# Layer norm without weights on one core: an in-place ring of 48 rows, and two-pass statistics on three engines

## The chip, the cores and the metric

The kernel runs on one core of one Trainium2 chip. The metric is the device time of one execution in microseconds; the number for a kernel is the median over its runs. Of the core's engines three compute here: VectorE (DVE in the profile), ScalarE (ACT) and GpSimd (POOL). SyncE (SP) and ScalarE issue DMAs. TensorE does nothing in either version.

## The reference

Every one of the 32 x 512 = 16384 vectors of 1024 fp32 numbers is brought to mean 0 and variance 1:

```python
def reference(x: np.ndarray, eps: float) -> np.ndarray:
    mean = np.mean(x, axis=-1, keepdims=True)
    var = np.var(x, axis=-1, keepdims=True)
    return ((x - mean) / np.sqrt(var + eps)).astype(np.float32)
```

x has the shape 32 x 512 x 1024, eps is 1e-5. 67.11 MB are read and 67.11 MB written.

## The kernel before

The 16384 vectors are cut into 128 "rows" of 128 vectors, one vector to each partition. A row is thus a 128x1024 piece of 0.52 MB, and a tile is K such rows: 15 tiles of 8 rows (4.19 MB each), then one of 4 and two of 2 rows. A tile is loaded by one DMA, and stored by one.

Input tiles go into `xr`, a ring of 32 rows, and results into `yr`, a ring of 16 rows, so up to four tiles of 8 are loaded ahead and two are on their way out. The instructions of each engine stand in the order in which the program writes them (`manual_schedule`); semaphores between engines and DMAs are set from the tiles that they read and write. Loads are issued on SP's queue, stores on ScalarE's.

For each tile `group` does the following:

- VectorE takes statistics over half rows of 512 elements (`bn_stats`, L77), two to a row, 16 to a tile of 8.
- GpSimd combines these half-row results into the sum of squared deviations and the negated mean, with nine small operations on at most 32 elements a partition (L66 to L102).
- ScalarE takes the square root (L105), VectorE the reciprocal (L109), GpSimd the product of negated mean and reciprocal (L111).
- ScalarE normalises each row (L113), from `xr` to `yr`, and issues the tile's store (L129).

A load into `xr` (L124) waits until ScalarE has read the rows that it overwrites; L113 waits until the store of the rows of `yr` that it overwrites has landed. What the change touches is all of `group`, the two rings, and the loop at the end of the kernel.

Of the kernel before, what the change touches and what calls it, by code (L numbers as in the profile page):

```python
# [1 line left out]

# [4 lines left out]


TILES = (8, 8, 8, 8, 8, 8, 8, 8, 8, 8, 8, 8, 8, 8, 8, 4, 2, 2)  # L10

XRING = 32
YRING = 16

GROUP = 8


def place(tiles, ring):

    plan, row, pos = [], 0, 0  # L20
    for K in tiles:
        if pos + K > ring:
            pos = 0
        plan.append((K, row, pos))
        row += K
        pos += K
    return plan


@with_exitstack  # L30
def kernel(
    ctx: ExitStack,
    tc: tile.TileContext,
    x: bass.AP,
    eps: bass.AP,
    out: bass.AP,
):
    nc = tc.nc
    P = nc.NUM_PARTITIONS
    eps_val = float(eps) if not isinstance(eps, bass.AP) else 1e-5  # L40

    x2 = x.flatten_outer_dims()
    o2 = out.flatten_outer_dims()
    N, D = x2.shape
    BN_MAX = nc.vector.BN_STATS_FMAX
    NSUB = D // BN_MAX
    assert sum(TILES) * P == N

    rings = ctx.enter_context(tc.tile_pool(name="rings", bufs=1))
    st = ctx.enter_context(tc.tile_pool(name="st", bufs=4))  # L50

    fdt = mybir.dt.float32
    AF = mybir.ActivationFunctionType
    ALU = mybir.AluOpType

    xr = rings.tile([P, XRING, D], fdt)
    yr = rings.tile([P, YRING, D], fdt)
    eps_t = rings.tile([P, 1], fdt)

    def rows_of(a, row, K):  # L60
        return a[row * P : (row + K) * P].rearrange("(p k) d -> p k d", p=P)

    def pool_sum(o, terms):
        G = terms.shape[1]
        half = st.tile([P, GROUP, 2], fdt, name="half")
        nc.gpsimd.tensor_tensor(  # L66
            out=half[:, :G], in0=terms[:, :, 0:2], in1=terms[:, :, 2:4], op=ALU.add
        )
        nc.gpsimd.tensor_tensor(  # L69
            out=o, in0=half[:, :G, 0], in1=half[:, :G, 1], op=ALU.add  # L70
        )

    def group(xs, ys, G):
        stats = st.tile([P, GROUP, NSUB, 6], fdt, name="stats")
        for k in range(G):
            for s in range(NSUB):
                nc.vector.bn_stats(  # L77
                    out=stats[:, k, s, :],
                    in_=xs[:, k, s * BN_MAX : (s + 1) * BN_MAX],
                )  # L80

        H = 2 * NSUB
        parts = stats[:, :G].rearrange("p g s (h c) -> p g (s h) c", h=2)
        mean4, m2 = parts[:, :, :, 1], parts[:, :, :, 2]
        nmean = st.tile([P, GROUP], fdt, name="nmean")
        dev = st.tile([P, GROUP, H], fdt, name="dev")
        ss = st.tile([P, GROUP], fdt, name="ss")
        pool_sum(nmean[:, :G], mean4)
        nc.gpsimd.tensor_scalar(  # L89
            out=nmean[:, :G], in0=nmean[:, :G], scalar1=-1.0 / H, scalar2=None, op0=ALU.mult  # L90
        )
        nc.gpsimd.tensor_tensor(  # L92
            out=dev[:, :G],
            in0=mean4,
            in1=nmean[:, :G].unsqueeze(2).to_broadcast([P, G, H]),
            op=ALU.add,
        )
        nc.gpsimd.tensor_mul(out=dev[:, :G], in0=dev[:, :G], in1=dev[:, :G])  # L98
        nc.gpsimd.tensor_scalar(  # L99
            out=dev[:, :G], in0=dev[:, :G], scalar1=float(D // H), scalar2=None, op0=ALU.mult  # L100
        )
        nc.gpsimd.tensor_tensor(out=dev[:, :G], in0=dev[:, :G], in1=m2, op=ALU.add)  # L102
        pool_sum(ss[:, :G], dev[:, :G])
        std = st.tile([P, GROUP], fdt, name="std")
        nc.scalar.activation(  # L105
            out=std[:, :G], in_=ss[:, :G], func=AF.Sqrt, bias=eps_t, scale=1.0 / D
        )
        rstd = st.tile([P, GROUP], fdt, name="rstd")
        nc.vector.reciprocal(out=rstd[:, :G], in_=std[:, :G])  # L109
        nmr = st.tile([P, GROUP], fdt, name="nmr")  # L110
        nc.gpsimd.tensor_mul(out=nmr[:, :G], in0=nmean[:, :G], in1=rstd[:, :G])  # L111
        for k in range(G):
            nc.scalar.activation(  # L113
                out=ys[:, k, :],
                in_=xs[:, k, :],
                func=AF.Identity,
                bias=nmr[:, k : k + 1],
                scale=rstd[:, k : k + 1],
            )

    with tc.manual_schedule():
        nc.vector.memset(eps_t, eps_val)  # L122
        for (K, row, xp), (_, _, yp) in zip(place(TILES, XRING), place(TILES, YRING)):
            nc.sync.dma_start(out=xr[:, xp : xp + K, :], in_=rows_of(x2, row, K))  # L124
            for g in range(0, K, GROUP):
                G = min(GROUP, K - g)
                a, b = xp + g, yp + g
                group(xr[:, a : a + G, :], yr[:, b : b + G, :], G)
            nc.scalar.dma_start(out=rows_of(o2, row, K), in_=yr[:, yp : yp + K, :])  # L129


# [1 line left out]
_INS = ['x', 'eps']  # L133
_OUTS = [((32, 512, 1024), 'float32')]

_NUMBERS = {'eps': 1e-05}


# [26 lines left out]
```

## Time and profile before

| | us |
|---|---|
| median of 12 runs (318.09 to 319.24) | 318.46 |
| the profiled execution's own time | 318.93 |
| its span, first to last instruction | 317.2 |
| time around the span | 1.7 |
| first load, issue to landing | 12.3 |
| a load of 4 MiB, issue to landing, median | 34.4 |
| a store of 4 MiB, issue to landing, median | 29.4 |

The page gives busy time for each engine, then 40 equal slices of the span with the busy share in tenths, the share of the 16 DMA engines and the rate in GB/s. A landing time holds the time in which a DMA shares the DMA engines with others in flight. The groups list, for each line of the kernel and operation, the shape, the count, the sum of the durations, the mean of one, and the idle time of the engine ahead of them with what ended it. A mean can be longer than the spacing, because one instruction's end overlaps the next one's start.

### The profile page before, as it was taken

Reading aid. Unit: us, or ns where it says so; the run is one execution under the profiler, and the core shown is the slowest. Engines: PE = TensorE matmul, PEld = TensorE weight load, DVE = VectorE, ACT = ScalarE, POOL = GpSimd, SP = SyncE. Lnnn points to the kernel's source line nnn. Section 1 sums busy time; section 2 is a strip of 40 time slices with the busy share of each in tenths; the row PEclk is TensorE's granted clock in tenths of the full one; section 3 lists DMA queues with packets and bytes.
Section 4 is the critical chain, followed back from the end, with each engine's and each line's share of the span. In section 5 each row is a group of like instructions: output and inputs, shape, how many; then the busy total and the mean of one; then the engine's idle time right before and its main releaser. Section 6 shows DMA issues by size and latency. Waiting matters only on the chain.

```text
span 317.2 us, 749 instructions
## 1 busy us (share of the span) xinstructions
DVE 155.6 (49%) x275; ACT 153.4 (48%) x147; POOL 41.2 (13%) x184
## 2 busy tenths in 40 slices
DVE  0387595709256191652907438083480925650330
ACT  1007591290833809247091651906529074759651
POOL 0011202200202002020020200102011020202220
DMA  8999999999999999999999999999999999999996
GB/s 331 409 450 434 413 402 438 430 430 430 434 427 446 417 426 443 434 430 442 426 434 426 434 434 439 422 442 434 430 434 426 438 434 432 432 422 439 421 413 257
DMA packets 5189, 134.26 MB, mean 423 GB/s; under 512 B 576, under 2 KB 576, under 8 KB 576
## 3 DMA queue, kind: packets, MB, share of 16 engines
q1 hardware_dynamic: 2592, 67.11, 49.6%
q10 hardware_dynamic: 2592, 67.11, 49.1%
q14 instruction: 5, 0.04, 0.0%
HBM read 67.11 MB, written 67.11 MB: 423 GB/s over the span
## 4 chain that ended last, share of the span: by engine, by line
DMA 64%; ACT 23%; DVE 7%; POOL 2%; issue 1%; ACTq 0%; POOLq 0%
DMA out_dram<-yr 61%; ACT yr L113 22%; DVE stats L77 7%; DMA xr<-in_x_dram 4%; POOL half L66 0%; ACT std L105 0%; POOL dev L99 0%; POOL dev L102 0%; POOL dev L92 0%; POOL nmean L89 0%; POOL dev L98 0%; POOL nmean L69 0%; POOL ss L69 0%; DVE rstd L109 0%; ACTq L129 0%
## 5 line engine op out<-in xcount | busy, mean ns | idle before, releaser
L113 ACT ACTIVATE yr<-xr,nmr,rstd 128x1024 f32<-128x1024 f32 x128 | 146.7, 1226 | 118.3 <-DMA out_dram<-yr 116.2
L77 DVE BATCH_NORM_STATS2 stats<-xr 128x6 f32<-128x512 f32 x256 | 153.3, 676 | 12.2 <-DMA xr<-in_x_dram 12.2
L109 DVE RECIPROCAL rstd<-std 128x8 f32<-128x8 f32 (+2 forms) x18 | 3.5, 197 | 138.9 <-ACT std L105 138.9
L66 POOL TENSOR_TENSOR half<-stats 128x16 f32<-128x16 f32 (+2 forms) x18 | 4.1, 230 | 161.3 <-DVE stats L77 161.3
L105 ACT ACTIVATE std<-ss,eps_t 128x8 f32<-128x8 f32 (+2 forms) x18 | 5.4, 300 | 37.4 <-POOL ss L69 31.4
L111 POOL TENSOR_TENSOR nmr<-nmean,rstd 128x8 f32<-128x8 f32 (+2 forms) x18 | 3.6, 200 | 93.2 <-DVE rstd L109 93.2
L99 POOL TENSOR_SCALAR dev<-dev 128x32 f32<-128x32 f32 (+2 forms) x18 | 5.2, 290 | 1.6
L102 POOL TENSOR_TENSOR dev<-dev,stats 128x32 f32<-128x32 f32 (+2 forms) x18 | 4.5, 250 | 1.5
L92 POOL TENSOR_TENSOR dev<-stats,nmean 128x32 f32<-128x32 f32 (+2 forms) x18 | 4.3, 237 | 1.5
L98 POOL TENSOR_TENSOR dev<-dev 128x32 f32<-128x32 f32 (+2 forms) x18 | 4.2, 233 | 1.4
L89 POOL TENSOR_SCALAR nmean<-nmean 128x8 f32<-128x8 f32 (+2 forms) x18 | 4.1, 229 | 1.6
L66 POOL TENSOR_TENSOR half<-dev 128x16 f32<-128x16 f32 (+2 forms) x18 | 3.8, 212 | 1.4
L69 POOL TENSOR_TENSOR nmean<-half 128x8 f32<-128x8 f32 (+2 forms) x18 | 3.6, 200 | 1.4
L69 POOL TENSOR_TENSOR ss<-half 128x8 f32<-128x8 f32 (+2 forms) x18 | 3.6, 200 | 1.4
L105 ACT ACT_TABLE_LOAD x1 | 1.3, 1283 | 0.9 <-DVE eps_t L122 0.9
L122 DVE MEMSET eps_t<- 128x1 f32 x1 | 0.1, 59 | 0.8 <-PEq L146 0.8
L146 POOL MEMSET const-float32-0.0<- 128x1 f32 x1 | 0.1, 98 | 0.2 <-issue 0.2
L146 POOL MEMSET const-bfloat16-1.0<- 128x1 bf16 x1 | 0.1, 101 | 0.0
L146 POOL MEMSET const-uint8-127<- 128x1 uint8 x1 | 0.1, 101 | 0.0
L146 POOL MEMSET const-float32-1.0<- 128x1 f32 x1 | 0.1, 98 | 0.0
## 6 DMA issues: line engine op xcount, KB each, us to landing
xr<-in_x_dram SPq DMA_DIRECT2D x15, 4096.0 KB, 34.4
out_dram<-yr ACTq DMA_DIRECT2D x15, 4096.0 KB, 29.4
xr<-in_x_dram SPq DMA_DIRECT2D x1, 2048.0 KB, 34.0
xr<-in_x_dram SPq DMA_DIRECT2D x2, 1024.0 KB, 47.0
out_dram<-yr ACTq DMA_DIRECT2D x1, 2048.0 KB, 10.1
out_dram<-yr ACTq DMA_DIRECT2D x2, 1024.0 KB, 7.4
```

Source lines behind the costliest of these rows:

```text
L66: nc.gpsimd.tensor_tensor(out=half[:, :G], in0=terms[:, :, 0:2], in1=terms[:, :, 2:4], op=ALU.add)
L69: nc.gpsimd.tensor_tensor(out=o, in0=half[:, :G, 0], in1=half[:, :G, 1], op=ALU.add)
L77: nc.vector.bn_stats(out=stats[:, k, s, :], in_=xs[:, k, s * BN_MAX : (s + 1) * BN_MAX],)
L89: nc.gpsimd.tensor_scalar(out=nmean[:, :G], in0=nmean[:, :G], scalar1=-1.0 / H, scalar2=None, op0=ALU.mult)
L92: nc.gpsimd.tensor_tensor(out=dev[:, :G], in0=mean4, in1=nmean[:, :G].unsqueeze(2).to_broadcast([P, G, H]), op=ALU.add,)
L98: nc.gpsimd.tensor_mul(out=dev[:, :G], in0=dev[:, :G], in1=dev[:, :G])
L99: nc.gpsimd.tensor_scalar(out=dev[:, :G], in0=dev[:, :G], scalar1=float(D // H), scalar2=None, op0=ALU.mult)
L102: nc.gpsimd.tensor_tensor(out=dev[:, :G], in0=dev[:, :G], in1=m2, op=ALU.add)
L105: nc.scalar.activation(out=std[:, :G], in_=ss[:, :G], func=AF.Sqrt, bias=eps_t, scale=1.0 / D)
L109: nc.vector.reciprocal(out=rstd[:, :G], in_=std[:, :G])
L111: nc.gpsimd.tensor_mul(out=nmr[:, :G], in0=nmean[:, :G], in1=rstd[:, :G])
L113: nc.scalar.activation(out=ys[:, k, :], in_=xs[:, k, :], func=AF.Identity, bias=nmr[:, k : k + 1], scale=rstd[:, k : k + 1],)
```

## The change

Two things are changed together.

**Ring and queues.** One ring of 48 rows replaces `xr` and `yr`; results are written over the inputs. The tiles are now 4, 4, fourteen of 8, then 6 and 2 rows. Loads are issued on ScalarE's queue, stores on SP's. Seven loads go out at the start (48 rows). Each later load is issued behind the work of the tile two after the last owner of its rows (`BEHIND`): behind tile t the load of tile t+4, which waits for the store of tile t-2.

**Statistics and normalisation.** The first two tiles and the last three (`bn`) take half-row statistics on VectorE, which also combines them (`bn_aggr`). The thirteen tiles between (`two_pass`) do it in two passes: VectorE sums each row (L65), GpSimd scales the sums to the negated mean (L71), ScalarE squares the deviation of every row (L76), for six of the rows into PSUM and for two with an accumulated sum, VectorE adds up the squares in PSUM (L89), ScalarE takes the root (L98), VectorE the reciprocal (L101). The rows are normalised on GpSimd (L103, L147), and only in the last two tiles on ScalarE. On each engine a tile's instructions still stand behind those of the tile before: in the program as built GpSimd's list repeats one L71 and eight L103, VectorE's two L65, three L89 and one L101, ScalarE's eight L76, one L98 and, from the fourth tile, one load.

```diff
-TILES = (8, 8, 8, 8, 8, 8, 8, 8, 8, 8, 8, 8, 8, 8, 8, 4, 2, 2)
-
-XRING = 32
-YRING = 16
-
-GROUP = 8
...
+TILES = (4, 4) + (8,) * 14 + (6, 2)
+
+RING = 48
+
+
+HEAD, TAIL = 2, 3
+
+BEHIND = 2
...
+    st = ctx.enter_context(tc.tile_pool(name="st", bufs=2))
+    sm = ctx.enter_context(tc.tile_pool(name="sm", bufs=len(TILES)))
+    ps = ctx.enter_context(tc.tile_pool(name="ps", bufs=2, space=bass.MemoryType.PSUM))
...
+    ring = rings.tile([P, RING, D], fdt)
+    junk = rings.tile([P, D], fdt)
...
+    def two_pass(xs, K):
+
+        sums, ssq, std, rstd, nmean = map(small, ("sums", "ssq", "std", "rstd", "nmean"))
+        half = K // 2
+        for a in (0, half):
+            nc.vector.tensor_reduce(
+                out=sums[:, a : a + half],
+                in_=xs[:, a : a + half, :],
+                axis=AX.X,
+                op=ALU.add,
+            )
+        nc.gpsimd.tensor_scalar(
+            out=nmean[:, :K], in0=sums[:, :K], scalar1=-1.0 / D, scalar2=None, op0=ALU.mult
         )
...
+        def square(o, k, total=None):
+            nc.scalar.activation(
+                out=o,
+                in_=xs[:, k, :],
+                func=AF.Square,
+                bias=nmean[:, k : k + 1],
+                scale=1.0,
+                accum_out=total,
+            )
+
+        def chunk(k):
+            sq = ps.tile([P, 2, D], fdt, name="sq")
+            for i in range(2):
+                square(sq[:, i, :], k + i)
+            nc.vector.tensor_reduce(
+                out=ssq[:, k : k + 2], in_=sq, axis=AX.X, op=ALU.add
+            )
+
+        chunk(0)
+        chunk(2)
+        for k in range(6, K):
+            square(junk, k, ssq[:, k : k + 1])
+        chunk(4)
+        nc.scalar.activation(
+            out=std[:, :K], in_=ssq[:, :K], func=AF.Sqrt, bias=eps_t, scale=1.0 / D
         )
...
+        nc.vector.reciprocal(out=rstd[:, :K], in_=std[:, :K])
+        for k in range(K):
+            nc.gpsimd.tensor_scalar(
+                out=xs[:, k, :],
+                in0=xs[:, k, :],
+                scalar1=nmean[:, k : k + 1],
+                scalar2=rstd[:, k : k + 1],
+                op0=ALU.add,
+                op1=ALU.mult,
+            )
+
+    def bn(xs, K, on_scalar):
...
+            nc.vector.bn_aggr(out=mv[:, k, :], in_=stats[:, k, :, :])
...
+        for k in range(K):
+            if on_scalar:
+                nc.scalar.activation(
+                    out=xs[:, k, :],
+                    in_=xs[:, k, :],
+                    func=AF.Identity,
+                    bias=nmr[:, k : k + 1],
+                    scale=rstd[:, k : k + 1],
+                )
+            else:
+                nc.gpsimd.tensor_scalar(
+                    out=xs[:, k, :],
+                    in0=xs[:, k, :],
+                    scalar1=mv[:, k, 0:1],
+                    scalar2=rstd[:, k : k + 1],
+                    op0=ALU.subtract,
+                    op1=ALU.mult,
+                )
...
+    after, owner = [], {}
+    for t, (K, row, pos) in enumerate(plan):
+        before = [owner[r] for r in range(pos, pos + K) if r in owner]
+        after.append(max(before) + BEHIND if before else -1)
+        owner.update((r, t) for r in range(pos, pos + K))
+
+    def load(done):
+        for t, (K, row, pos) in enumerate(plan):
+            if after[t] == done:
+                nc.scalar.dma_start(
+                    out=ring[:, pos : pos + K, :], in_=rows_of(x2, row, K)
+                )
 
     with tc.manual_schedule():
...
+        load(-1)
+        nc.gpsimd.memset(eps_t, eps_val)
+        for t, (K, row, pos) in enumerate(plan):
+            xs = ring[:, pos : pos + K, :]
+            left = len(TILES) - t
+            if t < HEAD or left <= TAIL:
+                bn(xs, K, on_scalar=left <= 2)
+            else:
+                two_pass(xs, K)
+            nc.sync.dma_start(out=rows_of(o2, row, K), in_=xs)
+            load(t)
```

## The prediction

> **What bounds the kernel now.** I read the page's head and its slices first, then the windows of engine busy time with the DMA share, then the chain of waits, then the groups by form.
>
> ```profile
> span 317.2 us, 749 instructions
> DVE 155.6 (49%) x275; ACT 153.4 (48%) x147; POOL 41.2 (13%) x184
> DMA  8999999999999999999999999999999999999996
> GB/s 331 409 450 434 413 402 438 430 430 430 434 427 446 417 426 443 434 430 442 426 434 426 434 434 439 422 442 434 430 434 426 438 434 432 432 422 439 421 413 257
> ```
>
> No engine is busy half of the span; the DMA engines are full in every slice but the first and the last. The windows (length, then DVE, ACT and POOL busy us, clock, DMA share, GB/s) agree:
>
> ```profile
> 120.00:160.00 40.00, 19.40 (x34) 20.17 (x20) 5.56 (x25) 1.00 1.00 433
> 300.00:317.00 17.00, 2.74 (x6) 6.35 (x7) 2.24 (x11) 1.00 0.81 344
> ```
>
> The plateau is 433 GB/s at share 1.00. A tile of 8 rows moves 4.19 MB in and 4.19 MB out, so a tile costs 8.39 / 0.433 = 19.4 us of DMA. All 134.26 MB cost 310 us, and the span is only 7 us more. The chain says the same, and its first piece gives the latency of a first load:
>
> ```profile
> DMA 64%; ACT 23%; DVE 7%; POOL 2%; issue 1%; ACTq 0%; POOLq 0%
> ...
> 0.72 12.29 DMA xr<-in_x_dram
> ```
>
> The load's 4.19 MB take 9.7 us at the plateau, so 2.6 us are fixed. Prices of the work, by form:
>
> ```profile
> L113 ACT ACTIVATE yr<-xr,nmr,rstd 128x1024 f32<-128x1024 f32 x128 | 146.7, 1226 | 118.3 <-DMA out_dram<-yr 116.2 <-POOL nmr L111 2.1
> L105 ACT ACTIVATE std<-ss,eps_t 128x8 f32<-128x8 f32 x15 | 4.5, 301 | 34.3 <-POOL ss L69 29.0 <-ACT yr L113 5.2
> L77 DVE BATCH_NORM_STATS2 stats<-xr 128x6 f32<-128x512 f32 x256 | 153.3, 676 | 12.2 <-DMA xr<-in_x_dram 12.2
> L109 DVE RECIPROCAL rstd<-std 128x8 f32<-128x8 f32 x15 | 3.0, 203 | 122.8 <-ACT std L105 122.8
> L99 POOL TENSOR_SCALAR dev<-dev 128x32 f32<-128x32 f32 x15 | 4.5, 299 | 1.3
> L89 POOL TENSOR_SCALAR nmean<-nmean 128x8 f32<-128x8 f32 x15 | 3.5, 231 | 1.3
> L89 POOL TENSOR_SCALAR nmean<-nmean 128x2 f32<-128x2 f32 x2 | 0.4, 220 | 0.2
> L99 POOL TENSOR_SCALAR dev<-dev 128x16 f32<-128x16 f32 x1 | 0.3, 257 | 0.1
> ```
>
> VectorE's 256 statistics come every 0.60 us (153.3 / 256), ScalarE's rows every 1.146 us (146.7 / 128); the longer means are single latencies. In each 19.4 us tile both have about 9 us to spare: a compute chain is free until it needs more than 19.4 us a tile.
>
> **What the Trainium skill says.** "ScalarE: Activation LUTs", section "What ACT_TABLE_LOAD costs": an ACTIVATE takes 186 ns + 0.833 ns an element, each pointer operand 93 ns more, and neighbours overlap by 93 ns. L113 has two pointers: 186 + 186 + 853 = 1225, and the trace has 1226; it agrees. "VectorE: DVE Perf Modes", "The perf-mode tier table": a tensor_reduce runs at one element a cycle (0.96 GHz) for any type. L77 agrees for its operation: 512 elements are 533 ns, so the spacing holds 64 ns of overhead. "GPSIMD Engine Reference", "Elementwise — side-by-side cycle accounting": a loop body with up to two operations is port-bound at 1.03 cycles an element at 1.2 GHz, a tight unrolled loop 1.8 cycles (512 elements in 769 ns). The trace has only tiny tensors. "SBUF — State Buffer", "Who interferes with whom": a tensor_reduce never contends with GpSimd; nothing in the trace tests it.
>
> **The change, part by part.**
>
> *Loads, ring and stores.* 48 rows may be on chip, loads go out on ScalarE's queue, stores on SP's. Seven loads (48 rows) are issued at once, 7 x 0.36 us (stores on ScalarE's queue now take 338 to 374 ns each), plus the table load of 1.28 us: done by about 4.5 us, before tile 0 has landed, so nothing. Tile 0 (4 rows, 2.1 MB) lands at 0.72 + 2.6 + 4.8 = 8.2 us, tile 1 at 13.0, tile 2 at 22.7. Later loads are issued behind the square root of tile t for tile t+4 and wait for store t-2, which went out more than a period before; alone it needs about 12 us, under traffic 29.4 us now. So the wait should be over. If not, the next tile's squares on ScalarE stand behind it and the excess is paid in full. A load has three periods to land.
>
> *Statistics.* The 180 small POOL operations, the 256 half-row statistics and 128 ScalarE normalisations mostly go. All sat beside DMA, so their removal gains nothing by itself. In their place thirteen tiles (2 to 14) get a cycle through three engines, in strict program order on each: VectorE sums tile t+1 only after tile t's reciprocal; GpSimd scales t+1's sums (nmean) only after it has normalised all 8 rows of t; ScalarE's squares need nmean; the reciprocal needs the squares. So from reciprocal to reciprocal there is one serial loop, with only one overlap: the sums (VectorE) beside the normalisation (GpSimd).
> - Sums: 2 x (4096/0.96 + 64 ns) + 0.08 = 8.74 us. From below 7.5, from above 9.6 (L77's 1.17 ns an element).
> - nmean: 0.23 (L89) + 0.07 = 0.30 us.
> - Eight squares, one pointer fewer than L113: 1.13 us alone, 1.04 back to back. Every second one in the built program waits for the one before it, 1.18 with the wait. 4 x 1.04 + 4 x 1.18 = 8.9, and two accumulator reads, not in the trace, 0 to 0.2 us each, taken at 0.2: 9.3 us. Bounds 8.3 to 9.9.
> - Last reduction, 2048 elements from PSUM: 2.13 + 0.2 + 0.05 = 2.4 us. The first two hide under later squares.
> - Square root 0.30, reciprocal 0.20, handing over 0.1: 0.6 us.
>
> The loop without its overlapped pair is 0.3 + 9.3 + 2.4 + 0.6 = 12.6 us, so the period is T = 12.6 + max(8.74, 8c), c being GpSimd's time for one 128x1024 row with two pointers. Even with c at nothing T is 21.3, over the 19.4 of DMA: the kernel stops being DMA-bound, whatever c is.
>
> *The price c.* The skill's port bound gives 0.88 + 0.2 (L89's fixed part) = 1.08 us. Its 1.8-cycle loop gives 1.54 + about 0.17 = 1.7. The trace's one-dimensional slope, (231 - 220)/6 = 1.83 ns an element, gives 2.1; L99's slope, (299 - 257)/16 = 2.63, gives 2.9, but L99 runs over rows of four, whose loop starts may be most of it. I take 1.7: the small rows exclude neither end, yet none shows a slope near 0.86 ns. It is an estimate from the page on GPSIMD. 8c = 13.6, T = 26.2.
>
> *Head.* Tile 0: eight statistics 4.8, four aggregations (not in the trace; 0.06 to 0.3, taken as the reciprocal's 0.2), then 0.6: 14.4. Tile 1 the same, 20.6. GpSimd finishes both by 28, under the sums of tile 2 (22.7 to 31.4). Reciprocal of tile 2: 31.4 + 12.6 = 44. Of tile 14: 44 + 12 x 26.2 = 358.5.
>
> *Tail.* Tile 15's statistics end 11.9 later, at 370.4 (16 x 0.6 + 8 x 0.2 + 0.7), but GpSimd is on tile 14 until 372.1 and normalises tile 15 until 385.7. Tiles 16 and 17 are normalised on ScalarE: 370.4 + 9.1 + 7.0 = 386.5 and 389, so they wait for nothing. Then 8.39 MB of stores remain: 19.4 + 2.6 = 22. Span 407.7; around the span lie 318.93 - 317.2 = 1.7 us. Sum 409 us. The sum is made against the profiled 318.93; the median 318.46 is 0.5 lower, far below the errors here. In short: 409 = 219 + 112c for c above 1.5.
>
> **Rivals.**
> *B: GpSimd at its port rate, VectorE's sums close the loop.* c = 1.08, T = 21.3: tile 14's reciprocal at 299.7, tile 15's statistics 311.6, normalised 320.3, stores 22.4: 342.7 + 1.7 = 344 us. For it: the skill's port bound; against it: the slopes of L89 and L99.
> *C: GpSimd much slower.* c = 2.1: 454 us. c = 2.9: 219 + 325 + 6 (tiles 0 and 1 then hold up nmean of tile 2) = 550 us. For it: L99's slope; against it: rows of four elements.
> *D, the other side: VectorE reduces at two elements a cycle.* Sums 4.4 instead of 8.74 and the last reduction 1.3 instead of 2.4: T = max(4.4, 8c) + 11.5. It decides from T below 19.4, that is with c below 1.0. Then DMA sets the pace: reciprocal 14 at about 38 + 12 x 19.4 = 271, 11.9 and 8 for tile 15, 22.4 for stores: 313 + 1.7 = 315 us. Against it: the skill's one element a cycle, L77's rate, and the need for c below every estimate.
>
> **How the numbers follow.** The chosen case (c 1.4 to 2.0, 376 to 443 us) 0.46; B with c up to 1.4 (335 to 376) 0.27; C (over 443) 0.23; D 0.04. The prediction is 409. The range, 338 to 458, covers the chosen case, almost all of B and the near part of C. The lead of the slow cases is structural: the serial loop needs over 19.4 us for any c. Faster by over 0.2% 0.03, within 0.2% (about what a measurement of this kernel can tell) 0.01, slower 0.96.
>
> **What would show it.** In the profile after: the DMA share below 1.0 in the middle slices; ScalarE's squares waiting for nmean thirteen times, about 8c + 0.6 us each; nmean starting right behind the eighth normalised row (in B, behind the sums); the spacing of the normalising rows reads c, that of the reciprocals T. I am wrong if the reciprocals come every 19.4 us with DMA full; if nmean runs ahead of the normalisation; or if ScalarE stands at a load's wait for a store.

## The result, and the profile after

The kernel after takes 385.08 us (median of 8 runs, 385.01 to 385.19), the kernel before in the same series 318.39 us: 1.2091 times as long (interval 1.2081 to 1.2102). The profiled execution's span is 383.4 us. Its page begins, with the columns of before:

```profile
span 383.4 us, 595 instructions
DVE 237.0 (62%) x157; ACT 131.8 (34%) x157; POOL 185.6 (48%) x138
DMA  8999999999899999999998999999898090720397
GB/s 313 450 434 436 395 434 438 438 379 421 349 428 376 400 401 363 390 379 383 379 390 379 424 397 362 403 362 403 345 421 383 0 438 0 321 116 0 144 415 317
```

There are fewer instructions and still no engine is full, yet DMA no longer sets the pace: the rate lies about 385 GB/s through the middle and falls to nothing in three slices near the end. That most digits remain 9 is a trap: a 9 stands for 90% or more, so the tenths hide a loss of one part in ten. The window that stood at 433 GB/s and a share of 1.00 before has now

```profile
120.00:160.00 40.00, 29.27 (x12) 15.11 (x18) 19.23 (x18) 1.00 0.94 381
```

The rate has fallen by more than the share, so it is the GB/s that tells. The chain has turned over. DMA held 64% of it; now:

```profile
POOL 44%; ACT 27%; issue 13%; DVE 8%; DMA 2%; POOLq 1%; ACTq 0%
```

Who waited for whom (total us, times, longest):

```profile
POOL ring L103 <- DVE rstd L101: 156.9, 13, 12.1
ACT sq L76 <- POOL nmean L71: 144.4, 13, 24.5
DVE ssq L89 <- ACT sq L76: 87.9, 26, 17.0
...
DVE mv L122 <- POOL ring L147: 19.9, 1, 19.9
```

The first three are a circle of waits, each engine for the next, thirteen times: once for every two-pass tile. One period of it, from the chain in order of time (start, length, what; pieces under 0.1 us are left out, and `junk` is where the two rows with an accumulated sum are written):

```profile
188.56 0.21 DVE rstd L101
188.86 8.58 POOL ring L103 x8
197.44 0.80 issue
198.25 0.24 POOL nmean L71
198.51 1.13 ACT sq L76
199.66 2.16 ACT sq L76 x2
201.85 1.12 ACT sq L76
202.97 1.17 ACT junk L76 x2
204.16 1.24 ACT junk L76 x2
205.40 1.01 ACT sq L76
206.44 1.13 ACT sq L76
207.59 2.30 DVE ssq L89
209.91 0.31 ACT std L98
210.25 0.21 DVE rstd L101
```

Eight rows normalised (9.4 us with the 0.8 of "issue"), then the scaling, then eight squares, the last reduction, the root and the reciprocal: 21.69 us from one reciprocal to the next, against 19.4 us of DMA for a tile. VectorE's sums (8.7 us) don't appear, because they lie beside the rows and end before them.

The surprise is in the groups. The same operation on the same shape has two prices:

```profile
L103 POOL TENSOR_SCALAR ring<-ring,nmean,rstd 128x1024 f32<-128x1024 f32 x104 | 122.4, 1194 | 156.9 <-DVE rstd L101 156.9
...
L147 POOL TENSOR_SCALAR ring<-ring,mv,rstd 128x1024 f32<-128x1024 f32 x16 | 60.2, 3781 | 17.8 <-DVE rstd L126 17.8
```

Taken by spacing (the group's busy time, in which overlaps count once, divided by the count), a row costs 122.4 / 104 = 1.18 us in the two-pass tiles and 60.2 / 16 = 3.76 us in tiles 0, 1 and 15. The timeline (start, length, engine, line, operation) shows where the slow ones stand:

```profile
16.34 30.11 POOL L147 TENSOR_SCALAR ring<-ring,mv,rstd 128x1024 f32<-128x1024 f32 x8 [15.54 <-DVE rstd L126]
...
46.42 0.25 POOL L71 TENSOR_SCALAR nmean<-sums 128x8 f32<-128x8 f32 x1
...
330.70 30.13 POOL L147 TENSOR_SCALAR ring<-ring,mv,rstd 128x1024 f32<-128x1024 f32 x8 [2.31 <-DVE rstd L126]
```

Tile 2's sums were ready at 32 us, but its nmean stands behind the slow rows on GpSimd until 46.4. At the end tile 15 holds GpSimd from 330.7 to 360.8 us; from 345 us until then DMA has nothing to move, and there lies the last of the three empty slices. (Tile 16 is ready at 346.6 us, but its store stands behind tile 15's on SP's queue.) The other two empty slices, about 297 to 307 and 316 to 326 us, belong to the loop: the last loads were issued at 275 us, and after them DMA only has one store a period, with a gap before the next.

So two questions: why has one operation two prices, and is it the order of the loop, and not the work in it, that sets 21.69 us?

### The profile page after: what moved, and what is told of

Its sections match the earlier page's. It is cut to its first block, busy times and chain, and to the rows that moved or that the text cites. A ratio compares the mean times of both kernels' runs of the same rounds, so it can differ in the third digit from the quotient of the medians.

```text
span 383.4 us, 595 instructions
## 1 busy us (share of the span) xinstructions
DVE 237.0 (62%) x157; ACT 131.8 (34%) x157; POOL 185.6 (48%) x138
## 4 chain that ended last, share of the span: by engine, by line
POOL 44%; ACT 27%; issue 13%; DVE 8%; DMA 2%; POOLq 1%; ACTq 0%
POOL ring L103 29%; ACT sq L76 19%; POOL ring L147 14%; ACT junk L76 7%; DVE ssq L89 7%; DMA ring<-in_x_dram 2%; POOLq L221 1%; ACT std L98 1%; POOL nmean L71 1%; DVE rstd L101 1%; ACT ring L139 0%; DVE stats L118 0%; ACTq L221 0%; DVE mv L122 0%; ACT std L123 0%
## 5 line engine op out<-in xcount | busy, mean ns | idle before, releaser
L103 POOL TENSOR_SCALAR ring<-ring,nmean,rstd 128x1024 f32<-128x1024 f32 x104 | 122.4, 1194 | 156.9 <-DVE rstd L101 156.9
L89 DVE TENSOR_REDUCE ssq<-sq 128x2 f32<-128x2048 f32 x39 | 88.1, 2288 | 87.9 <-ACT sq L76 87.9
L76 ACT ACTIVATE sq<-ring,nmean 128x1024 f32<-128x1024 f32 x78 | 85.8, 1111 | 145.7 <-POOL nmean L71 144.4
L65 DVE TENSOR_REDUCE sums<-ring 128x4 f32<-128x4096 f32 x26 | 113.2, 4393 | 0.9 <-DMA ring<-in_x_dram 0.9
L147 POOL TENSOR_SCALAR ring<-ring,mv,rstd 128x1024 f32<-128x1024 f32 x16 | 60.2, 3781 | 17.8 <-DVE rstd L126 17.8
L118 DVE BATCH_NORM_STATS2 stats<-ring 128x6 f32<-128x512 f32 x48 | 29.7, 661 | 8.6 <-DMA ring<-in_x_dram 8.6
L76 ACT ACTIVATE junk<-ring,nmean 128x1024 f32<-128x1024 f32 x26 | 29.6, 1140 | 0.4
L122 DVE BATCH_NORM_AGGREGATE mv<-stats 128x2 f32<-128x12 f32 x24 | 5.0, 208 | 20.7 <-POOL ring L147 19.9
L98 ACT ACTIVATE std<-ssq,eps_t 128x8 f32<-128x8 f32 x13 | 3.9, 301 | 30.7 <-DVE ssq L89 30.7
L139 ACT ACTIVATE ring<-ring,nmr,rstd 128x1024 f32<-128x1024 f32 x8 | 9.3, 1228 | 0.9 <-DVE nmr L129 0.9
L123 ACT ACT_TABLE_LOAD x1 | 1.3, 1283 | 14.4 <-DVE mv L122 14.4
L101 DVE RECIPROCAL rstd<-std 128x8 f32<-128x8 f32 x13 | 2.6, 203 | 4.8 <-ACT std L98 4.8
L76 ACT ACTIVATION_READ_ACCUMULATOR junk<-ring,nmean 128x1 f32 x26 | 4.9, 187 | 0.0
L71 POOL TENSOR_SCALAR nmean<-sums 128x8 f32<-128x8 f32 x13 | 3.0, 233 | 0.0
```

Source lines behind the costliest of these rows:

```text
L65: nc.vector.tensor_reduce(out=sums[:, a : a + half], in_=xs[:, a : a + half, :], axis=AX.X, op=ALU.add,)
L71: nc.gpsimd.tensor_scalar(out=nmean[:, :K], in0=sums[:, :K], scalar1=-1.0 / D, scalar2=None, op0=ALU.mult)
L76: nc.scalar.activation(out=o, in_=xs[:, k, :], func=AF.Square, bias=nmean[:, k : k + 1], scale=1.0, accum_out=total,)
L89: nc.vector.tensor_reduce(out=ssq[:, k : k + 2], in_=sq, axis=AX.X, op=ALU.add)
L98: nc.scalar.activation(out=std[:, :K], in_=ssq[:, :K], func=AF.Sqrt, bias=eps_t, scale=1.0 / D)
L101: nc.vector.reciprocal(out=rstd[:, :K], in_=std[:, :K])
```

## The experiments

**The slow rows.** L103 adds and multiplies, L147 subtracts and multiplies; L103's pointers are contiguous, L147's first one steps over mean/variance pairs; and VectorE works beside some of the slow rows. First only the operation is changed, then only the pointer:

```diff
-                    op0=ALU.subtract,
+                    op0=ALU.add,
```

> The kernel after, with op0 of the normalisation L147 (tiles 0, 1 and 15) changed from subtract to add; its mean is thus added there and not subtracted. Pointers, shapes and order stay. Theory S (the operation subtract is what makes an L147 row take 3.77 us against 1.18 us for an L103 row): L147 falls to 1.2 us, the reciprocal of tile 2 comes at 44 us in place of 58.6, tile 15 takes 9.4 us in place of 30.1, and the time is about 350 us. Theory P (the pointer into the mean/variance pairs is slow): L147 stays at 3.77 us, time 385 us. Theory V (VectorE's work beside it slows it): 3.77 us, 385 us.

350.2 us, a single run (before: 318.19 in these runs). The rows take 18.9 / 16 = 1.18 us:

```profile
L147 POOL TENSOR_SCALAR ring<-ring,mv,rstd 128x1024 f32<-128x1024 f32 x16 | 18.9, 1198 | 18.9 <-DVE rstd L126 18.9
```

```diff
+        if not on_scalar:
+            mean = small("mean")
+            nc.vector.tensor_copy(out=mean[:, :K], in_=mv[:, :K, 0])
...
-                    scalar1=mv[:, k, 0:1],
+                    scalar1=mean[:, k : k + 1],
```

> The kernel after, with subtract kept in L147 and its first pointer moved to a contiguous copy of the means, as L103's pointers are. Theory S (subtract): still 3.77 us a row, 385 us. Theory P (pointer into pairs): 1.2 us a row, about 350 us. Theory V (VectorE beside it): 3.77 us, 385 us.

384.63 us, a single run, and the rows are as slow as ever:

```profile
L150 POOL TENSOR_SCALAR ring<-ring,mean,rstd 128x1024 f32<-128x1024 f32 x16 | 60.2, 3781 | 17.8 <-DVE mean L129 17.8
```

The pointer does nothing. VectorE does nothing either, since in e1_bn_add it works beside the rows just as before. Between these two forms the operation alone decides. The same result can be had without a subtract, with -mean * rstd from one small VectorE operation (`nmr`, whose lines are left out here):

```diff
-                    scalar1=mv[:, k, 0:1],
-                    scalar2=rstd[:, k : k + 1],
-                    op0=ALU.subtract,
-                    op1=ALU.mult,
+                    scalar1=rstd[:, k : k + 1],
+                    scalar2=nmr[:, k : k + 1],
+                    op0=ALU.mult,
+                    op1=ALU.add,
```

> The kernel after, with the GpSimd rows of tiles 0, 1 and 15 written as x * rstd + (-mean * rstd): multiply, then add, both pointers contiguous. Same result, no subtract. Head: tiles 0 and 1 are normalised by about 27.5 us, so nmean of tile 2 follows the sums at 32 us and not GpSimd at 46.4: reciprocal of tile 2 at 44.5, 14 us earlier. Tail: tile 15 takes 9.4 us and not 30.1. Loop unchanged at 21.7 us. Sum under theory S or P: 350 us (346 to 354). If the head's 14 us are given back to DMA, which is then behind: 358 to 364.

350.51 us, 1.1016 times before (1.0997 to 1.1034). Tile 2's reciprocal starts at 43.90 us where it started at 58.44, and tile 15's rows take 9.46 us where they took 30.13: 14.5 + 20.7 = 35.2 us, of which 34.6 appear in the time. DMA took none of it back.

Is subtract slow, or are add and multiply quick? Four more forms in one kernel:

```diff
+            elif t == 0:
...
+                    scalar1=rstd[:, k : k + 1],
+                    scalar2=nmr[:, k : k + 1],
+                    op0=ALU.mult,
+                    op1=ALU.subtract,
...
+            elif t == 1:
...
+                    scalar1=nmr[:, k : k + 1],
+                    scalar2=None,
+                    op0=ALU.subtract,
...
+            elif k < 4:
...
+                    scalar1=rstd[:, k : k + 1],
+                    scalar2=None,
+                    op0=ALU.mult,
...
+            else:
...
+                    scalar1=nmr[:, k : k + 1],
+                    scalar2=rstd[:, k : k + 1],
+                    op0=ALU.max,
+                    op1=ALU.mult,
```

> GpSimd's price by operation, in the kernel of e3_bn_mult_add: tile 0 takes multiply then subtract, tile 1 one subtract alone, the first four rows of tile 15 one multiply alone, its last four maximum then multiply; the results of these rows are not the layer norm. If any subtract is slow: tile 0 3.8 us a row, tile 1 2.5 to 3.8. If a subtract is slow only as first operation: tile 0 1.2 us, tile 1 2.5 to 3.8. If add and multiply alone are quick: maximum then multiply is slow too, 3 us or more; else 1.2. Multiply alone: 1.0 to 1.2.

377.28 us, a single run. In the order multiply-subtract, maximum-multiply, multiply alone, subtract alone:

```profile
L146 POOL TENSOR_SCALAR ring<-ring,rstd,nmr 128x1024 f32<-128x1024 f32 x4 | 15.1, 3782 | 15.7 <-DVE nmr L128 15.7
L171 POOL TENSOR_SCALAR ring<-ring,nmr,rstd 128x1024 f32<-128x1024 f32 x4 | 15.1, 3774 | 0.0
L163 POOL TENSOR_SCALAR ring<-ring,rstd 128x1024 f32<-128x1024 f32 x4 | 11.3, 2846 | 2.3 <-DVE rstd L126 2.3
L155 POOL TENSOR_SCALAR ring<-ring,nmr 128x1024 f32<-128x1024 f32 x4 | 11.3, 2843 | 0.0
```

The expectation for the multiply alone, 1.0 to 1.2 us, missed: it takes 11.3 / 4 = 2.8 us. Subtract is nothing special. Of the seven forms run here, add-multiply and multiply-add are quick (1.18 us), every other pair takes 3.8 us, and one operation alone 2.8 us. A multiplication alone is more than twice as long as a multiplication and an addition together. Why the forms differ, no run shows.

**The loop.** Only the order of issue is changed: the sums and nmean of tile t+1 go in ahead of tile t's last reduction and of its normalisation (`ahead()` issues them). Every operation stays, the slow rows too. Only the place of the call is shown here:

```diff
         chunk(0)
         chunk(2)
+        nxt = ahead()
         for k in range(6, K):
             square(junk, k, ssq[:, k : k + 1])
         chunk(4)
```

> The kernel after, only the order changed: the row sums and nmean of tile t+1 are issued after the second chunk of tile t, so ahead of tile t's last reduction on VectorE and of its normalisation on GpSimd. Operations are the same. Theory L (the serial loop through three engines sets the period): by the measured durations VectorE then needs 2 x 2.2 + 8.7 + 2.3 + 0.5 and the wait for the first squares, some 18.4 us a tile, and the reciprocals come every 19.4 us, DMA's pace, or a little less while DMA has a backlog; head (58 us) and the slow rows of tile 15 stay: 340 to 352 us. Theory G (GpSimd and VectorE slow each other when both work on the ring, so that the order doesn't matter): period stays near 21.7, 380 us or more.

345.85 us, 1.0869 times before (1.0853 to 1.0885), 39 us less than the kernel after. The timeline of two neighbouring tiles:

```profile
100.61 0.20 DVE L106 RECIPROCAL rstd<-std 128x8 f32<-128x8 f32 x1 [0.37 <-ACT std L103]
100.72 4.45 ACT L80 ACTIVATE sq<-ring,nmean 128x1024 f32<-128x1024 f32 x4
100.91 9.45 POOL L108 TENSOR_SCALAR ring<-ring,nmean,rstd 128x1024 f32<-128x1024 f32 x8 [2.55 <-DVE rstd L106]
...
118.73 0.20 DVE L106 RECIPROCAL rstd<-std 128x8 f32<-128x8 f32 x1 [0.37 <-ACT std L103]
```

The squares of a tile now run beside the rows of the tile before, and the reciprocals come every 18.12 us. That is shorter than DMA's 19.4 us, so DMA is the bound again: from 209 us on, when the tiles loaded ahead are used up, the reciprocals come every 19.3 to 19.8 us, and the rate is at its plateau even before that, as the window of 160 to 200 us shows (length, then DVE, ACT, POOL, clock, DMA share, GB/s):

```profile
160.00:200.00 40.00, 34.85 (x14) 22.13 (x28) 23.12 (x22) 1.00 1.00 433
```

The order was the cause of the 21.69 us. GpSimd's rows are as quick as in the kernel after (122.8 / 104 = 1.18 us), although VectorE and ScalarE work on the ring beside them for longer.

**Both mended.** The order of e4_ahead with the rows of e3_bn_mult_add (both edits above, nothing else):

> The order of e4_ahead together with the multiply-add rows of e3_bn_mult_add; same result. Theory L (serial loop) and the slow subtract explain the whole loss: the loop then runs at 18.1 us where data is on chip, DMA becomes the bound again, and the time is 2.6 + 310 + a few us for the last rows: 316 to 322 us. Theory G (something else in the new statistics holds the DMA back, such as loads waiting on ScalarE's queue): 328 us or more.

321.96 us, 1.0118 times before (1.0101 to 1.0135): of the 66.7 us that the change cost, some 63 are explained by these two edits. Alone they gained 34.6 and 39.2 us, which is more than 63 in sum: with both, the DMA share is 1.00 from 40 to 300 us, and DMA bounds what the second edit can still gain.

**The ring alone.** The statistics and the normalisation of the kernel before, in the new ring (`group` is that of the kernel before; its body is left out here):

```diff
-            if t < HEAD or left <= TAIL:
-                bn(xs, K, on_scalar=left <= 2)
-            else:
-                two_pass(xs, K)
+            group(xs, K)
```

> One part of the change alone: the ring of 48 rows, in place, with the new tiles, loads on ScalarE's queue and stores on SP's, but the statistics and the normalisation on ScalarE as in the kernel before. Theory L: the loss lies in the statistics alone, and the ring is as fast as before or a little faster, since the last loads are issued earlier and DMA works up to the end: 314 to 319 us. Theory R (the ring or its queues cost something, for example loads waiting for stores in front of ScalarE's rows): 322 us or more.

318.72 us, 1.0006 times before (0.9996 to 1.0016): no difference. By themselves the ring and its queues cost nothing and bring nothing; the loss comes with the new statistics and normalisation.

**What e5_ahead_add still lacks.** It is DMA-bound and yet 3.2 us slower than e6_ring_alone. The later loads were moved to SP's queue, and then also one tile earlier:

```diff
-                nc.scalar.dma_start(
+                (nc.scalar if done < 0 else nc.sync).dma_start(
```

> e5_ahead_add with the later loads moved from ScalarE's queue to SP's, each behind the store of the same tile. In e5 the DMA share is 1.00 but the rate dips (344 GB/s from 220 to 224 us), ScalarE's squares wait 5.8 us for landing stores, and the span is 4.0 us longer than e6_ring_alone's. Theory A (ScalarE stands at the loads' waits and so delays the loop): without these waits 319 us or less. Theory Q (too few bytes are queued on the DMA, since a load is issued only one store ahead): a load goes out some 10 us later than in e5, so the dips grow: 323 us or more. If neither, 321 to 323 us.

321.5 us (1.0096 times before, 1.0073 to 1.0119).

```diff
-BEHIND = 2
+BEHIND = 1
```

> As e8_load_sp, and each load one tile earlier (BEHIND 1 in place of 2): behind store t the load of tile t+3, which waits for store t-1. SP then stands about 9 us a tile for that store, in time for the next one, which is ready after 19 us. Theory Q (too few bytes queued): the dips go and the time is 317 to 319.5 us. Theory A: equal to e8_load_sp. If the rate itself is lower with this mix of reads and writes, whatever is queued: 321 to 323 us.

320.84 us (1.0078, 1.0061 to 1.0095). (With BEHIND 1 the load behind the store of tile t is that of tile t+5, not t+3 as the expectation has it: the first one, tile 7's, stands behind store 2.) Neither theory is borne out: e8_load_sp can't be told from e5_ahead_add, and e9_load_sp_early gains about 1 us on it, not three. The windows of e9_load_sp_early, then of e6_ring_alone:

```profile
80.00:120.00 40.00, 35.36 (x14) 18.20 (x22) 19.56 (x19) 1.00 0.99 421
...
160.00:200.00 40.00, 35.36 (x15) 22.41 (x29) 23.61 (x23) 1.00 1.01 433
```

```profile
80.00:120.00 40.00, 19.59 (x34) 18.92 (x18) 5.61 (x25) 1.00 1.00 434
```

From 120 to 300 us both are at the plateau of 433 GB/s, so a rate that is lower throughout is not the reason either. e9_load_sp_early falls behind in two places. From 80 to 120 us it is 13 GB/s short: 0.52 MB, or 1.2 us at the plateau. And in the last of its page's 40 slices, 8 us long, it moves 165 GB/s where e6_ring_alone's has 251: 0.7 MB, or 1.5 us. Together that is the 2.7 us between the two spans (318.9 and 316.2). Why the rate is lower in these two places stays open. No version here beats the kernel before.

## Why the prediction came out as it did

Slower, and within the range: 385.08 us against 409 forecast and 338 to 458 stated. The path was right, and the price of GpSimd's rows was wrong; that the number came out as near as it did is luck. Point by point:

- *The serial loop* was right, and so was its reason: with the sums at 8.7 us no c could bring it under 19.4 us. The signs that the prediction named are there: a DMA share below 1.0, ScalarE's squares waiting for nmean thirteen times (10.0 us each in the loop, 24.5 at the head), and nmean right behind the eighth row. The terms beside c: sums 8.74 predicted, 8.70 measured; nmean 0.30, 0.26; squares 9.3, 9.08; last reduction 2.4, 2.32; root and reciprocal 0.6, 0.55. The period less GpSimd's rows was put at 12.6 us and is 12.3.
- *The price c* failed, and in both directions. It was put at 1.7 us for every row. In the loop it is 1.18 us, near rival B's port rate, so T is 21.69 and not 26.2: 12 periods are 54.1 us shorter. In tiles 0, 1 and 15 it is 3.76 us, above rival C's worst: the reciprocal of tile 2 comes 14.6 us later (58.65, not 44), and from tile 14's reciprocal to the end of tile 15's rows it takes 42.0 us where 27.2 were forecast, 14.8 more. The sum, 409 - 54.1 + 14.6 + 14.8, is 384.3. So the distance of 24 us is small only because two errors of one term offset each other. The step that failed is to give add-multiply and subtract-multiply rows one price. Rival B had the loop nearly right (21.3 us, though the rows' 9.4 us close it and not the sums' 8.7) and missed 41 us, most of it by the slow rows.
- *L99's slope* had been set aside with a guess: that the starts of rows of four elements are most of it. Two things speak against that. L99 is a multiply alone, and its slope gave 2.9 us a row; in e7_ops a multiply alone takes 2.8. And in the trace of before L99 at 8 elements takes 236 ns, where L89, which has no rows of four, takes 231 (the prediction shows L89's line, L99's is below). The trace of before thus held about the right price of one form, but of neither form that the change uses on whole rows; and L89, a multiply alone as well, had given 2.1 from a slope over six elements.

```profile
L99 POOL TENSOR_SCALAR dev<-dev 128x8 f32<-128x8 f32 x2 | 0.5, 236 | 0.2
```

- *The Trainium skill*, "GPSIMD Engine Reference", "Elementwise — side-by-side cycle accounting": the estimate from its port rate was near for add and multiply in one instruction (1.08 us estimated, 1.18 measured), and neither of its two rates fits the other forms (2.8 and 3.8 us). The estimate of 1.7 us from its 1.8-cycle loop is met by none of them. "VectorE: DVE Perf Modes", "The perf-mode tier table": VectorE reduces two rows of squares in PSUM, 2048 elements, in 2.29 us, and 4096 elements in SBUF in 4.39 us, about one element a cycle for both, as the table has it. That a tensor_reduce and GpSimd do not contend, which nothing in the trace of before tested, holds here: in the kernel after, where sums and rows lie side by side, the sums take 4.37 to 4.42 us and the rows 1.19 to 1.20 us (single durations, not spacing); in e4_ahead, where GpSimd is idle for most of the sums, 4.41 to 4.42 and 1.20 us.
- *Ring, loads and stores*: costing nothing was right (e6_ring_alone), and no wait of a load for a store holds ScalarE up in the kernel after. The table load was expected under the first load; it stands behind VectorE's last aggregation of tile 0, at 14.4 us, and puts its 1.28 us on the head's path.
- *The last stores*: 22 us forecast after tile 15's rows, 22.6 measured (360.8 to 383.4).
- *A wait that was not foreseen*: tile 17's statistics share a buffer with tile 15's, which GpSimd reads until 360.8, so VectorE stands for 19.9 us. It should cost nothing: the stores of tiles 15 and 16 go first, and DMA is at work on them (408 GB/s from 360.8 to 372 us) when tile 17 is ready at 365.6.

## What to carry to other kernels

Add up the dependent durations around the loop, through every engine and in the order of issue, before asking how busy an engine is: here each engine was at most 62% busy, and the loop still took 21.7 us where DMA needs 19.4. Issuing the next tile's first step ahead of this tile's last wait cured the loop without changing an operation. And do not carry a price from one form of an instruction to another: on GpSimd the pair of operations alone moved a row from 1.18 to 3.8 us, and a subtract can be written as a multiply and an add.

## What the runs showed of the hardware that was not expected

- GpSimd's tensor_scalar on 128x1024 fp32, by spacing: add-multiply and multiply-add 1.18 us; subtract-multiply, multiply-subtract and maximum-multiply 3.8 us; multiply alone and subtract alone 2.8 us. One operation more makes it faster where the two are an add and a multiply. Only these seven forms were run, and why they differ is open.
- ScalarE's square with an accumulated sum is followed by a read of the accumulator of 187 ns, partly overlapped; two such rows take 2.41 us (202.90 to 205.31 us in the timeline), where two rows into PSUM take 2.25.
